# A Trainium2 encoder block: residual seeded into accumulators by ScalarE, and a fourth summed product in two groups of down

## The chip, the cores and the metric

One Trainium2 chip; the kernel uses one of its NeuronCores. Counted is the time of one execution on the device in microseconds. The kernel before took 1141.77 us (median of three runs, 1141.67 to 1141.77).

## What is computed

One layer of an encoder on 256 tokens of width 2048, in fp32:

```python
x = x + jnp.concatenate([out_mla, out_diff], axis=-1) @ w_out[layer]
...
x = x + xo @ w_xo[layer]
hf = rms_norm(x, g_ffn[layer])
x = x + (jax.nn.silu(hf @ w_gate[layer]) * (hf @ w_up[layer])) @ w_down[layer]
return rms_norm(x, g_final)
```

The change touches the two wide products whose result is added onto the residual x: `w_out` (2048 by 2048) and the larger part of `w_down`, called down here (5632 by 2048; the hidden width is taken in one chunk of 512 and five of 1024, numbered 0 to 4 below). x is kept in SBUF as two tiles `x_res` of 128 tokens by 2048.

## The kernel before

**fp32 in three matmuls.** Each operand is split into a rounded high part and a low rest. `mm` (L97 to L101) issues h by h, h by l and l by h, each a matmul with 512 columns, onto one PSUM bank of 128 by 512. Weights come by DMA on SyncE's queue into `wraw` (three buffers). ScalarE casts them to the high part `wh` (L107), VectorE subtracts that from the raw value to give the low part `wl` (L108); `wh` and `wl` have four buffers of 1024 columns each. A buffer is written again only when the last matmul that reads it is done.

**Pairs, P and W.** `wide_project` (L254) multiplies 256 tokens by a block of weights 1024 columns wide; the contracted dimension is taken in pairs of 128 rows. One pair is a 2 by 2 block product. A pair of kind P does it plainly in 8 `mm` (24 matmuls), into four accumulators `accs[tt][oc]`, tt the token tile and oc the block of 512 columns. A pair of kind W uses a scheme with 7 products (21 matmuls): it needs sums of weight blocks (`tsum`, VectorE, L291, L295, L296), split too (the second pair of sums into `wh2` and `wl2`, one buffer each), and sums of activations (`summed_pair`, L237, tiles `forms` and `sums`). Three of its products go straight to accumulators, four into banks Q1, Q5, Q7, Q6, which are summed over all W pairs of a call. The four accumulators and the four Q banks are in two pools of four banks, which swap roles after each call (`banks.reverse()`, L326). The Q pool also serves the transposes `pt` (L504, and L924 in a chunk).

**Leaving and joining.** After the last W of a call, `leave(Q)` (L355) copies Q1 to SBUF on ScalarE (L357) and combines Q1, Q5, Q7, Q6 with the four blocks of x in eight VectorE operations of 128 by 512 (L358 to L365). At the end of the call `join` (L367) adds each accumulator onto x. `wide_add` (L349) is this form, with eight calls: two halves of 1024 columns for w_out; two halves each for three groups of down: chunk 0; chunks 1 and 2; chunks 3 and 4. Gate and up use `wide_result` (L329), which isn't changed.

**Kinds and order.** The two larger groups have eight pairs each: two P and two W from the first chunk (PPWW), and PPPW from the second. They are taken in the order 0, 1, 2, 4, 3, 6, 7, 5, so the W pairs 2, 3 and 7 stand at places 3, 5 and 7. In the second chunk's `wide_chunk` the third pair, being P, is split from the transposes into tiles `hT2`. The very last half-call (`DN_LAST`) takes only five pairs, one of them W; its other weights go through `weights` for a tail of plain products.

**What sets the order.** The program is emitted in the order of a schedule over all engines: each engine gets one static list of instructions and runs it in order, with waits on the other engines. The lists mix casts of weights to come, copies of PSUM and sums of chunks. Line numbers are those of the kernel before, save where the prediction and the order rows below name the changed kernel; there the seeds are L261, the sums of weights L287, L291, L292, the leave L357 to L361, the join L364.

Of the kernel before, what the change touches and what calls it, by code (L numbers as in the profile page):

```python
# [16 lines left out]
ALU = mybir.AluOpType  # L17
# [63 lines left out]
def encoder_block(ctx: ExitStack, tc: tile.TileContext, a, out):  # L81
# [12 lines left out]
    tp = tables.enter_context(tc.tile_pool(name="tp", bufs=1))  # L94


    def mm(o, l, r, start, stop):  # L97

        nc.tensor.matmul(o, l.h, r.h, start=start, stop=False)  # L99
        nc.tensor.matmul(o, l.h, r.l, start=False, stop=False)  # L100
        nc.tensor.matmul(o, l.l, r.h, start=False, stop=stop)  # L101

    last_split, last_cast = [None], [None]

# [146 lines left out]
        split_into(f[:, 4:8, :], s)  # L251
        return Pair(forms=f)

    def wide_project(pairs, src, order, kinds, leave, join, closed=(0, 1), before=None):  # L254

        accs = [[acc_tile() for _ in range(2)] for _ in range(NT)]
        used = [[False] * 2 for _ in range(NT)]
        summed = [i for i in order if kinds[i] == "W"]
        plain = [i for i in order if i not in summed]
        Q = {}
        for n, i in enumerate(order):
            stop = n == len(order) - 1  # L270
            if before is not None:
                before(n)
            raw = pair_raw(src[i])
            if i not in summed:
                w = [split_blocks(raw[:, 2 * k:2 * k + 2, :]) for k in range(2)]
                for tt in range(NT):
                    for oc in range(2):
                        for k in range(2):

                            ends = stop or i == plain[-1] and tt == oc == 1  # L280
                            mm(accs[tt][oc], pairs[i].at(k, tt), w[k][:, oc, :], not used[tt][oc],
                               ends and k == 1 and oc in closed)
                            used[tt][oc] = True
                continue
            if i == summed[0]:
                Q = {q: ps_tile(f"q{q}") for q in (1, 5, 7, 6)}

            b11 = split_blocks(raw[:, 1:3, :])
            if sum_pool:
                t = sum_pool[0].tile([P, 4, 512], F32, name="tsum", tag="tsum", bufs=1)  # L290
                nc.vector.tensor_tensor(out=t[:, 0:2, :], in0=raw[:, 1:3, :],  # L291
                                        in1=raw[:, 0:1, :].to_broadcast([P, 2, 512]), op=ALU.add)  # L292
                t13 = split_blocks(t[:, 0:2, :])
                b21 = split_blocks(raw[:, 3:4, :])
                nc.vector.tensor_tensor(out=t[:, 2, :], in0=t[:, 0, :], in1=raw[:, 2, :], op=ALU.add)  # L295
                nc.vector.tensor_tensor(out=t[:, 3, :], in0=t[:, 2, :], in1=raw[:, 3, :], op=ALU.add)  # L296
# [18 lines left out]
            mm(accs[0][1], S3, b11[:, 1, :], False, stop)  # L315
            mm(Q[5], S5, t1, *own)
            mm(Q[7], S7, t3, *own)
            mm(accs[0][0], A12, b21[:, 0, :], False, stop)
            mm(Q[6], S6, t2, *own)
            mm(accs[1][0], A22, t4, False, stop)  # L320
# [28 lines left out]
    def wide_add(pairs, src, order, kinds, oc0, done=None, closed=(0, 1), before=None):  # L349


        def x(tt, oc):
            return x_res[tt][:, (oc0 + oc) * 512:(oc0 + oc + 1) * 512]

        def leave(Q):  # L355
            v, u = nat("v"), nat("u")
            nc.scalar.copy(out=u, in_=Q[1])  # L357
            nc.vector.tensor_tensor(out=v, in0=Q[6], in1=u, op=ALU.subtract)  # L358
            nc.vector.tensor_tensor(out=x(0, 0), in0=x(0, 0), in1=Q[1], op=ALU.add)
# [12 lines left out]
        return wide_project(pairs, src, order, kinds, leave, join, closed, before)  # L372


    LAT = KVL + DR
# [558 lines left out]
    fss = small.tile([P, NT, 7], F32, name="fss", tag="fss", bufs=1)  # L934
    nc.gpsimd.memset(fss[:, :, 3:4], EPS)

    groups = [([0], (0, 1, 2, 4, 5, 3)), ([1, 2], (0, 1, 2, 4, 3, 6, 7, 5)), ([3, 4], (0, 1, 2, 4, 3, 6, 7, 5))]
    pair0 = 0
    for gi, (chunks, order) in enumerate(groups):
        hp = []  # L940
# [24 lines left out]

        wide_add(hp, src[0], order, kinds, 0, final_square)

        accs = wide_add(hp, src[1], (0, 2, 1, 3, 4), DN_LAST[-8:], 2, closed=(1,))
        summed_up = last_split[0]
        kts = [2 * i + k for i in (5, 6, 7) for k in range(2)]  # L970
        kt = 0
        for p in range(3):
            for w in weights(a["w_down"][0, p]):
                for tt in range(NT):
                    mm(accs[tt][0], xT(kts[kt])[tt], w, False, kt == 5)
# [5 lines left out]
        add_out([accs[tt][0] for tt in range(NT)], 2)  # L981
# [109 lines left out]
```

## Time and profile before

| What | us |
|---|---|
| median of three runs | 1141.77 |
| span of the profiled execution | 1140.2 |
| TensorE busy | 1131.5 |
| VectorE busy | 989.2 |
| ScalarE busy | 651.8 |
| GpSimd busy | 56.2 |

The profile is of one execution. The median is 1.57 us above its span: what lies ahead of the first and behind the last instruction. Times in a timeline are starts, counted from the span's start, followed by the length; a row may stand for several instructions (x2). Successive matmuls overlap, so the cost of one is read from start to start, not from its length.

### The profile page before, as it was taken

Reading aid. Unit: us, or ns where it says so; the run is one execution under the profiler, and the core shown is the slowest. Engines: PE = TensorE matmul, PEld = TensorE weight load, DVE = VectorE, ACT = ScalarE, POOL = GpSimd, SP = SyncE. Lnnn points to the kernel's source line nnn. Section 1 sums busy time; section 2 is a strip of 40 time slices with the busy share of each in tenths; the row PEclk is TensorE's granted clock in tenths of the full one; section 3 lists DMA queues with packets and bytes.
Section 4 is the critical chain, followed back from the end, with each engine's and each line's share of the span. In section 5 each row is a group of like instructions: output and inputs, shape, how many; then the busy total and the mean of one; then the engine's idle time right before and its main releaser. Section 6 shows DMA issues by size and latency. Waiting matters only on the chain.

```text
span 1140.2 us, 14409 instructions
## 1 busy us (share of the span) xinstructions
PE 1131.5 (99%) x5390; PEld 946.1 (83%) x5390; DVE 989.2 (87%) x1354; ACT 651.8 (57%) x933; POOL 56.2 (5%) x75
## 2 busy tenths in 40 slices
PE   9999999999999999999999999999999999999997
PEld 7888888888888888888888888888888888888876
DVE  7788766978997776989899998998999898998996
ACT  6755455556567555665555464564554664664653
POOL 4920000000001000000000000000000000000000
PEclk9999999999999999999999999999999999999999
DMA  9655334546557445455555555555555555565543
GB/s 349 243 196 186 132 118 145 181 142 228 207 209 274 150 156 185 160 210 188 215 191 216 180 198 214 185 195 211 185 202 205 209 197 196 192 243 204 192 170 133
DMA packets 35494, 222.14 MB, mean 195 GB/s; under 512 B 4320, under 2 KB 5600, under 8 KB 11104
## 3 DMA queue, kind: packets, MB, share of 16 engines
q1 hardware_dynamic: 33696, 216.60, 53.5%
q0 software_dynamic: 864, 3.15, 0.8%
q10 hardware_dynamic: 864, 1.47, 0.4%
q8 instruction: 42, 0.69, 0.2%
q14 instruction: 28, 0.23, 0.1%
HBM read 219.11 MB, written 2.10 MB: 194 GB/s over the span
## 4 chain that ended last, share of the span: by engine, by line
PE 98%; issue 0%; ACT 0%; DVE 0%; POOLq 0%; POOL 0%; ACTq 0%
PE acc L99 26%; PE acc L100 26%; PE acc L101 26%; PE q L99 4%; PE q L100 4%; PE q L101 4%; PE pt L504 2%; PE ppt L652 1%; PE psc L100 1%; PE psc L101 1%; PE psc L99 1%; PE acckv L99 0%; PE acckv L101 0%; PE acckv L100 0%; PE pt L924 0%
## 5 line engine op out<-in xcount | busy, mean ns | idle before, releaser
L107 ACT CAST wh<-wraw 128x1024 fp32r<-128x1024 f32 (+2 forms) x401 | 389.3, 989 | 330.4 <-PE acc L101 284.6
L108 DVE TENSOR_TENSOR wl<-wraw,wh 128x1024 fp32r<-128x1024 f32 (+2 forms) x401 | 455.5, 1151 | 82.6 <-ACT wh L107 81.0
L107 ACT CAST wh<-tsum 128x1024 fp32r<-128x1024 f32 (+1 forms) x98 | 98.5, 1007 | 53.4 <-PE acc L101 22.7
L108 DVE TENSOR_TENSOR wl<-tsum,wh 128x1024 fp32r<-128x1024 f32 (+1 forms) x98 | 114.1, 1168 | 13.8 <-ACT wh L107 13.8
L100 PE MATMUL acc<-wl,x2n_h 128*128 128x512 f32 x320 | 124.5, 390 | 0.0
L101 PE MATMUL acc<-wh,x2n_l 128*128 128x512 f32 x320 | 123.9, 389 | 0.0
L99 PE MATMUL acc<-wh,x2n_h 128*128 128x512 f32 x320 | 109.7, 390 | 0.0
L100 PE MATMUL acc<-wl,x0T_h 128*128 128x512 f32 x224 | 88.6, 395 | 0.0
L101 PE MATMUL acc<-wh,x0T_l 128*128 128x512 f32 x224 | 88.2, 394 | 0.0
L99 PE MATMUL acc<-wh,x0T_h 128*128 128x512 f32 x224 | 87.0, 397 | 0.0
L100 PE MATMUL q<-wl,forms_h 128*128 128x512 f32 x191 | 74.4, 390 | 0.0
L101 PE MATMUL q<-wh,forms_l 128*128 128x512 f32 x191 | 74.2, 389 | 0.0
L100 PE MATMUL acc<-wl,hT_h 128*128 128x512 f32 x188 | 73.1, 392 | 0.0
L101 PE MATMUL acc<-wh,hT_l 128*128 128x512 f32 x188 | 72.3, 390 | 0.0
L101 PEld LDWEIGHTS acc<-wh,x2n_l 128*128 128x128 f32 x320 | 60.1, 188 | 12.5
L100 PEld LDWEIGHTS acc<-wl,x2n_h 128*128 128x128 f32 x320 | 60.1, 188 | 12.3
L99 PEld LDWEIGHTS acc<-wh,x2n_h 128*128 128x128 f32 x320 | 59.9, 188 | 12.2
L99 PE MATMUL q<-wh,forms_h 128*128 128x512 f32 x191 | 67.2, 389 | 0.0
L99 PE MATMUL acc<-wh,hT_h 128*128 128x512 f32 x188 | 64.7, 391 | 0.0
L100 PE MATMUL acc<-wl,forms_h 128*128 128x512 f32 x162 | 63.0, 389 | 0.0
L101 PE MATMUL acc<-wh,forms_l 128*128 128x512 f32 x162 | 63.0, 389 | 0.0
L99 PE MATMUL acc<-wh,forms_h 128*128 128x512 f32 x162 | 61.2, 390 | 0.1
(406 smaller groups left out, 2252.6 us busy)
## 6 DMA issues: line engine op xcount, KB each, us to landing
wraw<-in_w_gate SPq DMA_DIRECT2D x44, 1024.0 KB, 4.8
wraw<-in_w_up SPq DMA_DIRECT2D x44, 1024.0 KB, 4.8
wraw<-in_w_dn SPq DMA_DIRECT2D x41, 1024.0 KB, 4.8
wraw<-in_w_in SPq DMA_DIRECT2D x24, 1024.0 KB, 4.8
wraw<-in_w_out SPq DMA_DIRECT2D x16, 1024.0 KB, 4.9
wraw<-in_w_in_lat SPq DMA_DIRECT2D x5, 832.0 KB, 7.1
wraw<-in_w_xk SPq DMA_DIRECT2D x4, 1024.0 KB, 4.9
wraw<-in_w_xq SPq DMA_DIRECT2D x4, 1024.0 KB, 5.0
```

The costliest lines, as they stand in the source:

```text
L99: nc.tensor.matmul(o, l.h, r.h, start=start, stop=False)
L100: nc.tensor.matmul(o, l.h, r.l, start=False, stop=False)
L101: nc.tensor.matmul(o, l.l, r.h, start=False, stop=stop)
L107: last_cast[0] = nc.scalar.copy(out=dst.h, in_=src).ins
L108: last_split[0] = nc.vector.tensor_tensor(out=dst.l, in0=src, in1=dst.h.bitcast(F32), op=ALU.subtract).ins
L504: nc.tensor.transpose(out=pt[:, j * P:(j + 1) * P], in_=src[:, j * P:(j + 1) * P], identity=ident)
L652: nc.tensor.transpose(out=pt[:, kt * S + tt * P:kt * S + (tt + 1) * P], in_=p[:, tt, kt * P:(kt + 1) * P], identity=ident)
```

## The change

`wide_add` hands `wide_project` its four blocks of x as seeds: ahead of a call's first matmul ScalarE copies each into its accumulator, and the matmuls add onto it (no matmul of these calls starts a fresh accumulation on those banks). `leave` then has the copy of Q1 and four VectorE operations, which leave the four combinations in SBUF tiles `left`; `join` adds accumulator and `left` and writes x. The last half-call's plain tail ends in the same `join`.

The kinds of the two larger groups become PPWWPPWW, and their order 0, 2, 1, 3, 4, 6, 7, 5, so the W pairs 2, 3, 6 and 7 stand at places 2, 4, 6 and 7. That makes three more W pairs (both halves of chunks 1 and 2, the first half of chunks 3 and 4), 5381 matmuls for 5390, 32 seed copies, and 32 vector operations fewer in `leave`; `hT2` is gone, and chunks 2 and 4 build the sums of one more pair.

```diff
-DN_KINDS = "PP" + "PPWW" + ("PPWW" + "PPPW") * (NPC // 2)
+DN_KINDS = "PP" + "PPWW" + ("PPWW" + "PPWW") * (NPC // 2)
...
-    def mm(o, l, r, start, stop):
+    def mm(o, l, r, start, stop, seeded=False):
-        nc.tensor.matmul(o, l.h, r.h, start=start, stop=False)
+        nc.tensor.matmul(o, l.h, r.h, start=start, stop=False, skip_group_check=seeded)
...
-    def wide_project(pairs, src, order, kinds, leave, join, closed=(0, 1), before=None):
+    def wide_project(pairs, src, order, kinds, leave, join, closed=(0, 1), before=None, seed=None):
         accs = [[acc_tile() for _ in range(2)] for _ in range(NT)]
-        used = [[False] * 2 for _ in range(NT)]
+        used = [[seed is not None] * 2 for _ in range(NT)]
+        if seed is not None:
+            for tt in range(NT):
+                for oc in range(2):
+                    nc.scalar.copy(out=accs[tt][oc], in_=seed(tt, oc))
...
+        sums = {}
+
         def leave(Q):
-            v, u = nat("v"), nat("u")
-            nc.scalar.copy(out=u, in_=Q[1])
-            nc.vector.tensor_tensor(out=v, in0=Q[6], in1=u, op=ALU.subtract)
-            nc.vector.tensor_tensor(out=x(0, 0), in0=x(0, 0), in1=Q[1], op=ALU.add)
+            for q in ((0, 0), (1, 0), (0, 1), (1, 1)):
+                sums[q] = nat("left")
+            q1, v, u, y = sums.values()
+            nc.scalar.copy(out=q1, in_=Q[1])
+            nc.vector.tensor_tensor(out=v, in0=Q[6], in1=q1, op=ALU.subtract)
             nc.vector.tensor_tensor(out=u, in0=Q[5], in1=v, op=ALU.add)
             nc.vector.tensor_tensor(out=v, in0=v, in1=Q[7], op=ALU.subtract)
-            nc.vector.tensor_tensor(out=x(1, 1), in0=x(1, 1), in1=Q[5], op=ALU.add)
-            nc.vector.tensor_tensor(out=x(0, 1), in0=x(0, 1), in1=u, op=ALU.add)
-            nc.vector.tensor_tensor(out=x(1, 0), in0=x(1, 0), in1=v, op=ALU.subtract)
-            nc.vector.tensor_tensor(out=x(1, 1), in0=x(1, 1), in1=v, op=ALU.add)
+            nc.vector.tensor_tensor(out=y, in0=Q[5], in1=v, op=ALU.add)
 
         def join(tt, oc, acc):
-            nc.vector.tensor_tensor(out=x(tt, oc), in0=x(tt, oc), in1=acc, op=ALU.add)
+            nc.vector.tensor_tensor(out=x(tt, oc), in0=acc, in1=sums[tt, oc],
+                                    op=ALU.subtract if (tt, oc) == (1, 0) else ALU.add)
...
-    groups = [([0], (0, 1, 2, 4, 5, 3)), ([1, 2], (0, 1, 2, 4, 3, 6, 7, 5)), ([3, 4], (0, 1, 2, 4, 3, 6, 7, 5))]
+    groups = [([0], (0, 1, 2, 4, 5, 3)), ([1, 2], (0, 2, 1, 3, 4, 6, 7, 5)), ([3, 4], (0, 2, 1, 3, 4, 6, 7, 5))]
```

In the last three products of a W and in P the new argument is passed to `mm`; the last half-call's `add_out` becomes a loop over `join`.

Three places of the lists are of use below, all in the first half of the group of chunks 1 and 2. In the names the number is that of the tile in its program, so the two programs number alike things differently; q1, q5, q7, q6 are the Q banks, acc the accumulators, and waits names the engines or DMA queues for which a row waits.

ScalarE around the copy of Q1, before:

```order
L107 CAST wh2_7473<-tsum_7461 128x1024 [waits PE_49]
L107 CAST wh_7540<-tsum_7538 128x1024 [waits DVE_49,PE_49,Activation_49]
L357 COPY u_7576<-q1_7376 128x512 [waits PE_49]
L107 CAST wh_7544<-wraw_7532 128x512 [waits PE_49,Activation_49]
L107 CAST wh2_7550<-tsum_7538 128x1024 [waits DVE_49,PE_49,Activation_49]
L107 CAST wh_7588<-wraw_7586 128x1024 [waits DMAHW4_49,PE_49]
L107 CAST wh_7592<-wraw_7586 128x1024 [waits PE_49]
```

and now:

```order
L107 CAST wh2_7537<-tsum_7525 128x1024 [waits DVE_49,Activation_49]
L357 COPY left_7605<-q1_7363 128x512 [waits PE_49]
L261 COPY acc_7652<-xres0_111 128x512 [waits Activation_49]
L107 CAST wh_7570<-tsum_7568 128x1024 [waits DVE_49]
L107 CAST wh_7574<-wraw_7562 128x512
L107 CAST wh_7616<-wraw_7614 128x1024 [waits DMAHW4_49]
L107 CAST wh_7620<-wraw_7614 128x1024 [waits PE_49]
L107 CAST wh2_7580<-tsum_7568 128x1024 [waits DVE_49,PE_49]
```

The seed of the first accumulator of the next half (acc_7652, first block of x) now stands directly behind the copy, and behind it the casts of the last W's sums and of the P that follows; the cast for wh2 has moved from behind the copy to ahead of it for one W, and far behind it for the next.

TensorE from the last matmul onto Q1, before:

```order
L101 MATMUL q1_7376<-wh_7534,forms_l_7288 128x512
L100 MATMUL acc_7303<-wl_7535,forms_h_7287 128x512
L101 MATMUL acc_7303<-wh_7534,forms_l_7288 128x512
L100 MATMUL q6_7379<-wl2_7474,forms_h_6596 128x512 [waits DVE_49]
L101 MATMUL q6_7379<-wh2_7473,forms_l_6597 128x512
L100 MATMUL acc_7304<-wl2_7474,forms_h_6596 128x512
L101 MATMUL acc_7304<-wh2_7473,forms_l_6597 128x512
L99 MATMUL acc_7304<-wh_7500,hT2h_7253 128x512
L100 MATMUL acc_7304<-wl_7501,hT2h_7253 128x512
L101 MATMUL acc_7304<-wh_7500,hT2l_7254 128x512
L99 MATMUL acc_7304<-wh_7504,hT2h_7253 128x512
L100 MATMUL acc_7304<-wl_7505,hT2h_7253 128x512
```

and now:

```order
L101 MATMUL q1_7363<-wh_7564,forms_l_7305 128x512
L100 MATMUL acc_7320<-wl_7565,forms_h_7304 128x512
L101 MATMUL acc_7320<-wh_7564,forms_l_7305 128x512
L100 MATMUL q6_7366<-wl2_7538,forms_h_7289 128x512 [waits DVE_49]
L101 MATMUL q6_7366<-wh2_7537,forms_l_7290 128x512
L100 MATMUL acc_7321<-wl2_7538,forms_h_7289 128x512
L101 MATMUL acc_7321<-wh2_7537,forms_l_7290 128x512
L99 MATMUL q5_7364<-wh_7570,forms_h_7304 128x512 [waits Activation_49]
L99 MATMUL q7_7365<-wh_7570,forms_h_7304 128x512
L99 MATMUL acc_7319<-wh_7574,forms_h_7304 128x512 [waits Activation_49]
L99 MATMUL acc_7320<-wh_7616,hT_h_7259 128x512 [waits Activation_49]
L99 MATMUL acc_7322<-wh_7616,hT_h_7259 128x512
```

Two W pairs now run interleaved here. Between the last matmul onto Q1 and the first use of the casts behind the copy (wh_7570, wh_7574, wh_7616; before wh_7544, still after these rows) there are six, eight and nine matmuls.

TensorE between two uses of the single wh2 buffer, before, where the next wh2 tile (wh2_7473) comes 24 matmuls after the last reader of wh2_7396:

```order
L99 MATMUL q6_7379<-wh2_7396,forms_h_6581 128x512 [waits DVE_49]
L100 MATMUL q6_7379<-wl2_7397,forms_h_6581 128x512
L101 MATMUL q6_7379<-wh2_7396,forms_l_6582 128x512
L99 MATMUL acc_7302<-wh_7467,forms_h_6596 128x512 [waits Activation_49]
L100 MATMUL acc_7302<-wl_7468,forms_h_6596 128x512 [waits DVE_49]
```

and now, with wh2_7383 and wh2_7460:

```order
L99 MATMUL q7_7365<-wh_7450,forms_h_6604 128x512
L100 MATMUL q7_7365<-wl_7451,forms_h_6604 128x512
L101 MATMUL q7_7365<-wh_7450,forms_l_6605 128x512
L99 MATMUL q6_7366<-wh2_7383,forms_h_6589 128x512 [waits DVE_49]
L100 MATMUL q6_7366<-wl2_7384,forms_h_6589 128x512
L101 MATMUL q6_7366<-wh2_7383,forms_l_6590 128x512
L99 MATMUL q1_7363<-wh_7521,forms_h_7289 128x512 [waits Activation_49]
L99 MATMUL acc_7320<-wh_7521,forms_h_7289 128x512
L99 MATMUL q6_7366<-wh2_7460,forms_h_6604 128x512 [waits Activation_49]
```

The products of pair 2 onto q7 and q6 have moved to directly ahead of those of pair 3 and of the next W.

More of the change, by code (lines that the diff above doesn't have):

```diff
@@ L94, in encoder_block @@
     tp = tables.enter_context(tc.tile_pool(name="tp", bufs=1))
-    def mm(o, l, r, start, stop):
-        nc.tensor.matmul(o, l.h, r.h, start=start, stop=False)
-        nc.tensor.matmul(o, l.h, r.l, start=False, stop=False)
-        nc.tensor.matmul(o, l.l, r.h, start=False, stop=stop)
+    def mm(o, l, r, start, stop, seeded=False):
+        nc.tensor.matmul(o, l.h, r.h, start=start, stop=False, skip_group_check=seeded)
+        nc.tensor.matmul(o, l.h, r.l, start=False, stop=False, skip_group_check=seeded)
+        nc.tensor.matmul(o, l.l, r.h, start=False, stop=stop, skip_group_check=seeded)
     last_split, last_cast = [None], [None]
@@ L281, in wide_project @@
                             mm(accs[tt][oc], pairs[i].at(k, tt), w[k][:, oc, :], not used[tt][oc],
-                               ends and k == 1 and oc in closed)
+                               ends and k == 1 and oc in closed, seed is not None)
                             used[tt][oc] = True
@@ L314, in wide_project @@
             mm(Q[1], A11, b11[:, 0, :], *own)
-            mm(accs[0][1], S3, b11[:, 1, :], False, stop)
+            mm(accs[0][1], S3, b11[:, 1, :], False, stop, seed is not None)
             mm(Q[5], S5, t1, *own)
             mm(Q[7], S7, t3, *own)
-            mm(accs[0][0], A12, b21[:, 0, :], False, stop)
+            mm(accs[0][0], A12, b21[:, 0, :], False, stop, seed is not None)
             mm(Q[6], S6, t2, *own)
-            mm(accs[1][0], A22, t4, False, stop)
+            mm(accs[1][0], A22, t4, False, stop, seed is not None)
             if i == summed[-1]:
@@ L353, in x @@
             return x_res[tt][:, (oc0 + oc) * 512:(oc0 + oc + 1) * 512]
+        sums = {}
         def leave(Q):
-            v, u = nat("v"), nat("u")
-            nc.scalar.copy(out=u, in_=Q[1])
-            nc.vector.tensor_tensor(out=v, in0=Q[6], in1=u, op=ALU.subtract)
-            nc.vector.tensor_tensor(out=x(0, 0), in0=x(0, 0), in1=Q[1], op=ALU.add)
+            for q in ((0, 0), (1, 0), (0, 1), (1, 1)):
[3 more added lines that the diff above has]
+            nc.vector.tensor_tensor(out=v, in0=Q[6], in1=q1, op=ALU.subtract)
             nc.vector.tensor_tensor(out=u, in0=Q[5], in1=v, op=ALU.add)
             nc.vector.tensor_tensor(out=v, in0=v, in1=Q[7], op=ALU.subtract)
-            nc.vector.tensor_tensor(out=x(1, 1), in0=x(1, 1), in1=Q[5], op=ALU.add)
-            nc.vector.tensor_tensor(out=x(0, 1), in0=x(0, 1), in1=u, op=ALU.add)
-            nc.vector.tensor_tensor(out=x(1, 0), in0=x(1, 0), in1=v, op=ALU.subtract)
-            nc.vector.tensor_tensor(out=x(1, 1), in0=x(1, 1), in1=v, op=ALU.add)
+            nc.vector.tensor_tensor(out=y, in0=Q[5], in1=v, op=ALU.add)
         def join(tt, oc, acc):
-            nc.vector.tensor_tensor(out=x(tt, oc), in0=x(tt, oc), in1=acc, op=ALU.add)
+            nc.vector.tensor_tensor(out=x(tt, oc), in0=acc, in1=sums[tt, oc],
+                                    op=ALU.subtract if (tt, oc) == (1, 0) else ALU.add)
             if done is not None:
                 done(tt, oc0 + oc)
-        return wide_project(pairs, src, order, kinds, leave, join, closed, before)
+        accs = wide_project(pairs, src, order, kinds, leave, join, closed, before, x)
+        return accs, join
     LAT = KVL + DR
@@ L966, in encoder_block @@
         wide_add(hp, src[0], order, kinds, 0, final_square)
-        accs = wide_add(hp, src[1], (0, 2, 1, 3, 4), DN_LAST[-8:], 2, closed=(1,))
+        accs, join = wide_add(hp, src[1], (0, 2, 1, 3, 4), DN_LAST[-8:], 2, closed=(1,))
         summed_up = last_split[0]
@@ L974, in encoder_block @@
                 for tt in range(NT):
-                    mm(accs[tt][0], xT(kts[kt])[tt], w, False, kt == 5)
+                    mm(accs[tt][0], xT(kts[kt])[tt], w, False, kt == 5, True)
                 kt += 1
@@ L980, in encoder_block @@
                     final_gain(tt, oc)
-        add_out([accs[tt][0] for tt in range(NT)], 2)
+        for tt in range(NT):
+            join(tt, 0, accs[tt][0])
         for tt in range(NT):
```

## Prediction

> **What bounds the kernel now.** First the page: its span, the engines' shares, the granted clock in 40 slices and the chain that ended last.
>
> ```profile
> span 1140.2 us, 14409 instructions
> PE 1131.5 (99%) x5390; PEld 946.1 (83%) x5390; DVE 989.2 (87%) x1354; ACT 651.8 (57%) x933; POOL 56.2 (5%) x75
> PEclk9999999999999999999999999999999999999999
> PE 98%; issue 0%; ACT 0%; DVE 0%; POOLq 0%; POOL 0%; ACTq 0%
> ```
>
> TensorE works without pause at full clock, so a matmul taken out pays in full, and a wait put in costs in full. Nothing else is late by more than fractions of a microsecond. The profiled span is 1140.2 us; the median of the three runs is 1141.77 us, so 1.57 us lie outside the span, and I add all changes to 1141.77.
>
> Next the busy time by stage, for the stages that gain summed products: 793 to 838 us holds most of down's first half in the group of chunks 1 and 2, 838 to 882 what follows it, 1046 to 1097 the same place in the last group.
>
> ```profile
> core 0: us, PE busy (x) PEld busy (x) DVE busy (x) ACT busy (x) POOL busy (x), PEclk, DMA share, GB/s
> 793.00:838.00 45.00, 45.00 (x208) 37.35 (x207) 42.37 (x55) 26.35 (x33) 0.00 (x0) 1.00 0.56 198
> 838.00:882.00 44.00, 44.00 (x196) 36.44 (x195) 40.42 (x48) 21.40 (x23) 0.00 (x0) 1.00 0.53 193
> 1046.00:1097.00 51.00, 50.89 (x233) 41.95 (x232) 48.38 (x63) 29.31 (x39) 0.00 (x0) 1.00 0.48 173
> ```
>
> VectorE is busy for 42.37 of 45 and 48.38 of 51 us: 2.6 us of room in each. ScalarE has room on average, but its queue is in order: what stands behind a waiting copy waits too.
>
> The prices come from the timeline around the copy of Q1 in the first of these stages: TensorE, then ScalarE, then VectorE.
>
> ```profile
> 824.48 0.39 PE L100 MATMUL q<-wl,forms_h 128*128 128x512 f32 x1
> 824.71 0.39 PE L101 MATMUL q<-wh,forms_l 128*128 128x512 f32 x1
> 824.93 0.39 PE L100 MATMUL acc<-wl,forms_h 128*128 128x512 f32 x1
> 825.16 0.39 PE L101 MATMUL acc<-wh,forms_l 128*128 128x512 f32 x1
> ```
>
> ```profile
> 825.13 0.59 ACT L357 COPY u<-q 128x512 f32<-128x512 f32 x1 [0.65 <-PE q L101]
> 825.64 0.62 ACT L107 CAST wh<-wraw 128x512 fp32r<-128x512 f32 x1
> 826.54 1.05 ACT L107 CAST wh<-tsum 128x1024 fp32r<-128x1024 f32 x1 [0.27 <-DVE xres L359]
> 827.50 3.95 ACT L107 CAST wh<-wraw 128x1024 fp32r<-128x1024 f32 x4
> ```
>
> ```profile
> 819.70 1.22 DVE L108 TENSOR_TENSOR wl<-wraw,wh 128x1024 fp32r<-128x1024 f32 x1
> 820.84 1.22 DVE L108 TENSOR_TENSOR wl<-tsum,wh 128x1024 fp32r<-128x1024 f32 x1
> 824.07 0.69 DVE L296 TENSOR_TENSOR tsum<-tsum,wraw 128x512 f32<-128x512 f32 x1
> 824.68 1.22 DVE L108 TENSOR_TENSOR wl<-tsum,wh 128x1024 fp32r<-128x1024 f32 x1
> 825.82 0.68 DVE L359 TENSOR_TENSOR xres<-xres,q 128x512 f32<-128x512 f32 x1
> 826.42 0.68 DVE L108 TENSOR_TENSOR wl<-wraw,wh 128x512 fp32r<-128x512 f32 x1
> 827.62 1.23 DVE L108 TENSOR_TENSOR wl<-tsum,wh 128x1024 fp32r<-128x1024 f32 x1 [0.52 <-ACT wh L107]
> ```
>
> Read from start to start: a matmul 0.227; on ScalarE 0.51 for 512 columns (825.13 to 825.64) and 0.96 for 1024 (826.54 to 827.50, 1.05 to its end); on VectorE 0.60 for 512 (825.82 to 826.42) and 1.14 for 1024 (819.70 to 820.84, 1.22 to its end). From the last matmul onto Q1 (824.71) to ScalarE's copy (825.13) pass 0.42, and from a cast's start (826.54) to VectorE's low part (827.62) 1.08. So a buffer of 1024 columns that TensorE lets go is used again at the earliest 0.42 + 1.05 + about 0.05 = 1.53 us after the start of its last reader.
>
> **The change, part by part.**
>
> *Nine matmuls fewer.* Three pairs go from 24 to 21 matmuls each: 9 x 0.227 = **-2.04 us**, if nothing is late.
>
> *Four vector adds fewer in each of eight calls.* Each call sheds 4 x 0.60 = 2.4 us of VectorE. In most stages TensorE doesn't wait for it, and this is worth nothing. In w_out's second half it does wait:
>
> ```profile
> 327.65 0.39 PE L101 MATMUL q<-wh,forms_l 128*128 128x512 f32 x1
> 327.88 0.61 PE L99 MATMUL acc<-wh,mT_h 128*128 128x512 f32 x2
> 328.68 0.50 PE L100 MATMUL acc<-wl,mT_h 128*128 128x512 f32 x1 [0.19 <-DVE wl L108]
> 329.01 0.39 PE L101 MATMUL acc<-wh,mT_l 128*128 128x512 f32 x1
> ```
>
> ```profile
> 326.81 0.68 DVE L359 TENSOR_TENSOR xres<-xres,q 128x512 f32<-128x512 f32 x1
> 327.40 1.22 DVE L108 TENSOR_TENSOR wl<-wraw,wh 128x1024 fp32r<-128x1024 f32 x1
> ```
>
> Four matmuls take 1.36 us instead of 0.91, because the low part of 327.40 stands behind L359. That add goes, the low part comes 0.60 earlier: **-0.45 us**. Next late there would be the cast of the same weight, but the two matmuls from 327.88 on already run from it.
>
> *The copy of Q1 ahead of a cast, in the last half.* There the trace already shows what a ScalarE queue behind the Q1 copy can do:
>
> ```profile
> 1093.78 0.39 PE L101 MATMUL q<-wh,forms_l 128*128 128x512 f32 x1
> 1095.59 0.39 PE L101 MATMUL acc<-wh,hT_l 128*128 128x512 f32 x1
> 1095.82 0.99 PE L99 MATMUL acc<-wh,forms_h 128*128 128x512 f32 x2
> 1096.65 0.40 PE L99 MATMUL q<-wh,forms_h 128*128 128x512 f32 x1
> ```
>
> ```profile
> 1094.20 0.59 ACT L357 COPY u<-q 128x512 f32<-128x512 f32 x1 [3.04 <-PE q L101]
> 1094.68 0.62 ACT L107 CAST wh<-wraw 128x512 fp32r<-128x512 f32 x1
> 1095.20 1.05 ACT L107 CAST wh<-tsum 128x1024 fp32r<-128x1024 f32 x1
> ```
>
> Copy, cast and cast end at 1096.25, and the matmul pair at 1095.82 takes 0.83 instead of 0.45. In the changed order this second cast (wh2_9794) stands ahead of the copy, so it isn't held: **-0.38 us**. So far -2.87 us.
>
> *32 seed copies on ScalarE.* No copy from SBUF to PSUM by ScalarE is in the trace. The nearest row is the opposite direction, in the view of that line:
>
> ```profile
> L357 ACT COPY u<-q x8: 574/587/589, 277.4 to 1094.2; 128x512 f32<-128x512 f32 x8
> ```
>
> I take 0.51 in a queue, as from 825.13 to 825.64; the bounds are 0.3 (half) and 0.7. The Trainium skill's "ScalarE: Activation LUTs" (What ACT_TABLE_LOAD costs) gives an instruction with immediates 186 ns + 0.833 ns a column, less about 93 ns back to back: by that page an estimated 613 and 520 ns at 512 columns, against the 587 and 0.51 us here. Its tip that ScalarE reaches PSUM faster than SBUF speaks for the lower bound; no run here shows it yet, and by it the sum would be at most some 0.4 us lower.
>
> A seed costs where TensorE waits for what is queued behind it. Most of the 32 stand behind the join that frees their value and 1 to 2 us or more ahead of their first matmul: nothing. One in each of the two large groups does not: acc_7652 and acc_9730, the seed of the first accumulator of the next half, directly behind the Q1 copy.
>
> *That place, counted from the start of the last matmul onto Q1 (time 0).* Before, behind the copy stood a 512-column cast used only 15 matmuls (3.4 us) on. Now: copy from 0.42 to 0.93, seed to 1.44, then wh_7570 (ends 2.49), wh_7574 (starts 2.40, with 512 columns ends 3.0), wh_7616 (starts 2.91, ends 3.96). TensorE reaches their first matmuls at 7, 9 and 10 x 0.227 = 1.59, 2.04 and 2.27. So it waits 0.9, then hardly, then 0.75: **+1.7 us**, of which 0.5 is the seed. The same rows stand in the last group (wh_9640, wh_9644, wh_9686): **+1.7 us** again.
>
> *The first W, now second in the order, is held.* Its products Q7 and Q6 wait for chunk 2's sums, since their PSUM pool holds the transposes until these are read, and so come just ahead of those of the second W. That pair's wh2_7460 needs the single wh2 buffer, whose last reader is the last matmul of q6 from wh2_7383; TensorE asks for wh2_7460 three matmuls later, 0.68 us, where 1.53 are needed: **+0.85 us** a group, so +1.7. Before, 24 matmuls (5.4 us) lay between, and it was free. A low part on VectorE at the same place (wl_7488) may add up to 0.5 us a group; I leave it to the range.
>
> *VectorE's queue in the group of chunks 1 and 2.* A W instead of a P adds 1.14 + 2 x 0.60 for the sums of weights and 1.14 + 0.60 for low parts: 4.08 us. The extra form costs an estimated 1.4 (from 0.60 and 1.14 by width: 0.2 for 128 and 0.33 for 256 columns; four sums and 1024 columns of low parts against 512). Less the 2.4 of the adds this is +3.1 us in each first half, while TensorE's work shrinks by 0.68: 42.37 + 3.1 = 45.5 against 44.3 us. Row by row: wl_7571 starts at 1.44 + 1.08 = 2.52; with it to wl_7701 stand seven of 1024 columns (7 x 1.14), six of 512 (6 x 0.60) and the last (1.22): ready at 15.3. TensorE asks for it after 53 matmuls, 12.0. So 3.3 late in all, 1.7 of which it has waited already: **+1.6 us**. The last group's counterpart comes to 14.7 against 60 matmuls, 13.6: covered by the wait of 1.7. In the second halves the addition is 4.08 - 2.4 = 1.7 against 3.6 us of room: nothing.
>
> *Joins, DMAs, outputs.* Four joins a call stay; they now read seed-fed accumulators and a left tile, same width. Weights are the same transfers, and the queues' order around them the same: nothing. The tail behind the last matmul is unchanged.
>
> **Sum:** -2.87 + 2 x 1.7 + 2 x 0.85 + 1.6 = +3.8 us: 1141.77 + 3.8 = **1145.5 us**.
>
> **The rivals.** A difference below 0.2% (2.28 us) can't be told from none here.
>
> *No new wait decides (faster).* If these casts are ready in time, only the savings remain: 1141.77 - 2.87 = 1138.9 us. For it: TensorE was never held in these stages before, and ScalarE is half idle (26.35 of 45). Against it: the waits come from the order of an in-order queue, and the rows at 1095.82 show one. It decides if the three casts behind the copy wait for nothing TensorE needs within 2.3 us, or TensorE is already later than VectorE there for another reason. Chance 0.12.
>
> *Only the waits on ScalarE, not VectorE's queue (no change).* VectorE could reach wl_7701 in time if it enters the stage with more room, shed in earlier calls: -2.87 + 5.1 = 1144.0 us, and with seeds at 0.3 us 1143.5. Chance 0.20.
>
> *VectorE bounds both groups (slower still).* The 2.6 us of idling in each window are waits for casts; if they stay, the windows need 42.37 + 2.6 + 3.1 = 48.1 against 44.3 and 54.1 against 50.3 us: +3.8 in each, 1141.77 - 2.87 + 7.6 = 1146.5, and with 0.5 us a group for wl_7488 and the late casts of the next half up to 1149. Chance 0.14.
>
> *The clock falls in the pauses.* If a pause lets the granted clock drop to a half for as long again as it lasted, the pauses of 1.7, 1.6, 1.7 and twice 0.85 us cost half their 6.7 us more: 1148.9 us. For it, nothing: the clock stands at 1.00 in every window. The Trainium skill's "TensorE: Matmul & The Clock Gate" (What's actually happening) drops the clock after an idle window of about 3.4 us; none of these pauses is that long, so by it this doesn't happen. Chance 0.04.
>
> **How the numbers follow.** The forecast itself has 0.50, from 1144.1 to 1147.5 us: seeds of 0.3 take 0.4 off, wl_7488 adds up to 1.0, VectorE's term may be 0.5 to 2.2. The range leaves out the faster case and the ends of the two slowest: 1142.0 to 1148.5 us. Faster 0.12; the second rival is "same", 0.20; the rest, 0.68, is slower.
>
> **What would show it.** Right: TensorE pauses of some 0.9 and 0.75 us right behind the last matmul onto Q1 in both large groups, released by ScalarE's casts; 0.85 at the second W's first matmul from wh2; a pause for a low part at the start of the second half in the first group only; none at 328 and 1095.8 us any more; seeds of about 0.59 us. Wrong: no pauses there, or pauses in places that I held free (w_out, chunk 0's group, the second halves), or a clock under 1.00.

## The result and the profile after

The changed kernel takes **1153.29 us** (median of four runs, 1152.99 to 1153.82), against 1141.77 us: a ratio of 1.0101, 95% interval 1.0088 to 1.0113. It was forecast slower at 1145.5 us with a range up to 1148.5: the way was right, but the change is about three times as large as forecast and lies beyond the range. The span of the profiled execution grew from 1140.2 to 1151.4 us.

The page of the changed kernel, the same lines as before:

```profile
span 1151.4 us, 14427 instructions
PE 1133.1 (98%) x5381; PEld 942.8 (82%) x5381; DVE 989.0 (86%) x1347; ACT 673.7 (59%) x975; POOL 57.9 (5%) x75
PEclk9999999999999999999999999999999999999999
PE 92%; DVE 4%; ACT 2%; issue 1%; DMA 1%; POOLq 0%; POOL 0%; DVEq 0%; ACTq 0%
```

Nine matmuls fewer, and VectorE's busy time over the whole is the same (989.2 before, 989.0 now): what the shorter leave saved, the fourth W took. The chain that ended last is no longer TensorE's alone; VectorE has 4% and ScalarE 2% of it. What TensorE waited for, by the view of its waits:

```profile
PE q L99 <- ACT wh L107: 3.9, 6, 0.9
PE q L100 <- DVE wl L108: 2.0, 1, 2.0
PE acc L99 <- ACT acc L261: 1.9, 2, 1.1
...
PE acc L100 <- DVE wl L108: 0.9, 2, 0.6
PE acc L99 <- ACT wh L107: 0.9, 2, 0.5
```

The columns are the total, the times and the longest. This view counts idle time between matmuls whose ends are modelled; what a wait costs is read from start to start, less 0.227 us for each matmul. The timeline of TensorE shows where, in the first half of the group of chunks 1 and 2:

```profile
813.78 0.51 PE L100 MATMUL acc<-wl,hT_h 128*128 128x512 f32 x1 [0.30 <-DVE wl L108]
...
819.65 0.40 PE L99 MATMUL acc<-wh,forms_h 128*128 128x512 f32 x1
820.66 0.50 PE L99 MATMUL q<-wh,forms_h 128*128 128x512 f32 x1 [0.62 <-ACT wh L107]
...
824.89 0.40 PE L99 MATMUL acc<-wh,forms_h 128*128 128x512 f32 x1
825.73 0.50 PE L99 MATMUL q<-wh,forms_h 128*128 128x512 f32 x1 [0.44 <-ACT wh L107]
...
829.72 0.39 PE L101 MATMUL acc<-wh,forms_l 128*128 128x512 f32 x1
831.02 0.73 PE L99 MATMUL q<-wh,forms_h 128*128 128x512 f32 x2 [0.92 <-ACT wh L107]
831.60 0.45 PE L99 MATMUL acc<-wh,forms_h 128*128 128x512 f32 x1
832.50 0.73 PE L99 MATMUL acc<-wh,hT_h 128*128 128x512 f32 x2 [0.45 <-ACT wh L107]
...
842.15 0.39 PE L99 MATMUL q<-wh,forms_h 128*128 128x512 f32 x1
844.58 0.50 PE L100 MATMUL q<-wl,forms_h 128*128 128x512 f32 x1 [2.05 <-DVE wl L108]
844.92 0.39 PE L101 MATMUL q<-wh,forms_l 128*128 128x512 f32 x1
```

From 844.58 to 844.92 are 0.34 us: the matmul behind a wait takes 0.11 more than its 0.227, at every wait of this list. With that, the waits here cost 0.91 (for low parts, around 813), 0.78 + 0.11, 0.61 + 0.11, 1.07 + 0.11, 0.67 + 0.11 and 2.20 + 0.11: 6.8 us. The last group has the first five too, from 1070 to 1092 us (4.9 us, with 1.28 for the low parts), and another at its second half. That one and one in w_out wait for seeds:

```profile
287.44 0.39 PE L99 MATMUL acc<-wh,mixT_h 128*128 128x512 f32 x1
288.58 0.50 PE L99 MATMUL acc<-wh,mixT_h 128*128 128x512 f32 x1 [0.74 <-ACT acc L261]
...
1100.78 0.39 PE L99 MATMUL q<-wh,forms_h 128*128 128x512 f32 x1
1102.32 0.50 PE L99 MATMUL acc<-wh,hT_h 128*128 128x512 f32 x1 [1.15 <-ACT acc L261]
```

They cost 0.91 + 0.11 and 1.31 + 0.11 us. ScalarE's timeline shows what stood ahead of the first of the two: two casts, then a mean square (L206) that needs the join of the half before, then the seed.

```profile
285.42 2.00 ACT L107 CAST wh<-wraw 128x1024 fp32r<-128x1024 f32 x2 [1.21 <-issue]
287.33 0.62 ACT L206 ACTIVATE junk<-xres 128x512 bf16<-128x512 f32 x1
287.86 0.18 ACT L206 ACTIVATION_READ_ACCUMULATOR junk<-xres 128x1 f32 x1
287.95 0.57 ACT L261 COPY acc<-xres 128x512 f32<-128x512 f32 x1
```

All together: 6.8 + 6.3 for the groups, 1.0 + 0.3 in w_out (0.27 ahead of the seed's wait, at 280 us), less 2.0 for the matmuls and 0.5 + 0.4 for the old waits at 328 and 1095.8 us, which are gone: +11.5, against 11.2 us of span. The waits are where the extra time is; the experiments ask why they are there.

### The profile page after: what moved, and what is told of

The parts are those of the page before. It is cut to its first block, busy times and chain, and to the rows that moved or that the text cites. A ratio compares the mean times of both kernels' runs of the same rounds, so it can differ in the third digit from the quotient of the medians.

```text
span 1151.4 us, 14427 instructions
## 1 busy us (share of the span) xinstructions
PE 1133.1 (98%) x5381; PEld 942.8 (82%) x5381; DVE 989.0 (86%) x1347; ACT 673.7 (59%) x975; POOL 57.9 (5%) x75
## 4 chain that ended last, share of the span: by engine, by line
PE 92%; DVE 4%; ACT 2%; issue 1%; DMA 1%; POOLq 0%; POOL 0%; DVEq 0%; ACTq 0%
PE acc L99 24%; PE acc L100 24%; PE acc L101 24%; PE q L100 4%; PE q L101 4%; PE q L99 4%; DVE wl L108 2%; PE pt L502 2%; ACT wh L107 1%; DMA wraw<-in_w_dn 1%; DVE tsum L287 1%; PE ppt L650 1%; PE psc L100 1%; PE psc L101 1%; PE psc L99 1%
## 5 line engine op out<-in xcount | busy, mean ns | idle before, releaser
L107 ACT CAST wh<-tsum 128x1024 fp32r<-128x1024 f32 (+1 forms) x104 | 104.2, 1009 | 61.7 <-PE acc L101 24.3
L108 DVE TENSOR_TENSOR wl<-tsum,wh 128x1024 fp32r<-128x1024 f32 (+1 forms) x104 | 120.8, 1168 | 14.1 <-ACT wh L107 13.7
L100 PE MATMUL q<-wl,forms_h 128*128 128x512 f32 x203 | 79.0, 390 | 2.0 <-DVE wl L108 2.0
L101 PE MATMUL q<-wh,forms_l 128*128 128x512 f32 x203 | 78.8, 389 | 0.0
L99 PE MATMUL q<-wh,forms_h 128*128 128x512 f32 x203 | 72.3, 393 | 3.9 <-ACT wh L107 3.9
L100 PE MATMUL acc<-wl,forms_h 128*128 128x512 f32 x175 | 68.1, 391 | 0.1
L101 PE MATMUL acc<-wh,forms_l 128*128 128x512 f32 x175 | 67.6, 389 | 0.0
L99 PE MATMUL acc<-wh,forms_h 128*128 128x512 f32 x175 | 66.9, 392 | 0.0
```

The costliest lines, as they stand in the source:

```text
L99: nc.tensor.matmul(o, l.h, r.h, start=start, stop=False, skip_group_check=seeded)
L100: nc.tensor.matmul(o, l.h, r.l, start=False, stop=False, skip_group_check=seeded)
L101: nc.tensor.matmul(o, l.l, r.h, start=False, stop=stop, skip_group_check=seeded)
L107: last_cast[0] = nc.scalar.copy(out=dst.h, in_=src).ins
L108: last_split[0] = nc.vector.tensor_tensor(out=dst.l, in0=src, in1=dst.h.bitcast(F32), op=ALU.subtract).ins
```

## The experiments

**First theory**, that of the prediction: the new order and kinds put waits into the in-order queues at particular places (behind the copy of Q1, at the one wh2 buffer). **Second**: VectorE's work bounds the groups. **Third**: the seeds themselves hold ScalarE and TensorE.

The lists of every run are emitted anew from its own schedule. An edit therefore also moves rows that it doesn't name, and no run has exactly the order of the change.

**Seeds alone.** The old kinds and order, the rest of the change kept:

```diff
-DN_KINDS = "PP" + "PPWW" + ("PPWW" + "PPWW") * (NPC // 2)
+DN_KINDS = "PP" + "PPWW" + ("PPWW" + "PPPW") * (NPC // 2)
-    groups = [... ([1, 2], (0, 2, 1, 3, 4, 6, 7, 5)), ([3, 4], (0, 2, 1, 3, 4, 6, 7, 5))]
+    groups = [... ([1, 2], (0, 1, 2, 4, 3, 6, 7, 5)), ([3, 4], (0, 1, 2, 4, 3, 6, 7, 5))]
```

> The seeds, the shorter leave and the new join, with the old kinds (three W pairs of eight) and the old order. First theory (the time is lost in waits that the new kinds and order put into the in-order queues of ScalarE and VectorE; seeds cost only where one stands late): the seed wait at w_out's second half (1.0 us) stays, the two old pauses at 328 and 1095.8 us go, so 1141.0 to 1143.5 us. Second theory (VectorE's total work bounds the groups): less work than before, so at most 1141.5 us. Third theory (the seed copies themselves hold ScalarE and TensorE): most of the 11.5 us stays, 1148 us or more.

Measured 1141.86 us, ratio 1.0001 (0.9992 to 1.0011): no change. The third theory falls, and the second's "at most 1141.5" is missed by 0.4 us. 32 seeds and 32 vector operations fewer, VectorE's busy time down from 989.2 to 973.5 us, and nothing gained: TensorE wasn't waiting for it. The late seed in w_out is there (1.0 us, at 289) and eats what the old two waits give back.

**Fourth W and order alone.** The kernel before with only these two lines changed, without seeds:

> The fourth W and the new order, with the old leave, join and no seeds. First theory: the waits at the early W, at the wh2 buffer, at the sums and behind the copy of Q1 stay, each without the 0.5 us of the seed, and the late seeds (1.0 and 1.4 us) go: 1148 to 1151 us. Second theory: VectorE has 2.4 us more to do in each call than in the changed kernel, so slower than 1153 us, up to 1158. Third theory: without seeds only the saved matmuls count, 1139 to 1142 us.

Measured 1151.31 us, ratio 1.0084 (1.0069 to 1.0099): just above the first theory's 1151. So most of the loss is with the fourth W or its order. The second theory, as stated, expected slower than 1153. It misses: VectorE does 15.6 us more here than in the change (1004.6 for 989.0) and the kernel is 2.0 us faster. The adds that the leave sheds are worth little; in the half shown above, seven of the eight operations of the long leave come behind the W pairs, from 840 us on.

**The old order with four W:**

```diff
-    groups = [... ([1, 2], (0, 2, 1, 3, 4, 6, 7, 5)), ([3, 4], (0, 2, 1, 3, 4, 6, 7, 5))]
+    groups = [... ([1, 2], (0, 1, 2, 4, 3, 6, 7, 5)), ([3, 4], (0, 1, 2, 4, 3, 6, 7, 5))]
```

> The changed kernel with the groups' old order 0, 1, 2, 4, 3, 6, 7, 5; seeds and the fourth W stay, so the matmuls and VectorE's work are those of the changed kernel. First theory: the pauses that come from the W at place 2 (some 0.9 to 1.3 for low parts, 0.9 for wh2, 0.7 for the sums, in each group) go, one or two waits behind the copy of Q1 stay: 1146 to 1149 us. Second and third theory: the same work and the same seeds, so still 1152 to 1154 us.

Measured 1153.44 us, ratio 1.0103 (1.0088 to 1.0118): the first theory misses, by 4 us and more; the second and third expected 1152 to 1154. TensorE's waits by this view:

```profile
PE q L99 <- ACT wh L107: 5.3, 7, 1.2
PE acc L99 <- ACT acc L261: 1.9, 2, 1.1
PE acc L99 <- ACT wh L107: 1.3, 3, 0.5
...
PE q L100 <- DVE wl L108: 1.1, 2, 0.5
```

The waits of the early W are gone, and others, of the same sum, are in places that were free.

**Two buffers for wh2:**

```diff
-        pool, tags, bufs = (wp, ("wh", "wl"), 4) if pool is None else (pool, ("wh2", "wl2"), 1)
+        pool, tags, bufs = (wp, ("wh", "wl"), (4, 4)) if pool is None else (pool, ("wh2", "wl2"), (2, 1))
```

> The changed kernel with two buffers for the tile wh2 (wl2 still one). First theory: the pause of 0.90 us a group at the first use of wh2 goes, everything else stays: 1151.0 to 1152.0 us, unless the wait for the sums behind it grows by the same amount. Second and third theory: no change, 1153 us.

Measured 1152.07 us, ratio 1.009 (1.0073 to 1.0107): about 1.2 us less than the change, just short of the 1.3 to 2.3 that the first theory expected. The wait of 0.90 for wh2 went, but just behind its place TensorE now waits 0.68 us for a low part, so only 0.2 us a group is gained there; the rest comes from other places of the new lists.

**Alternating pairs.** The first theory in a mended form, that W pairs side by side are the trouble, and a **new theory** against it:

```diff
-    groups = [... ([1, 2], (0, 2, 1, 3, 4, 6, 7, 5)), ([3, 4], (0, 2, 1, 3, 4, 6, 7, 5))]
+    groups = [... ([1, 2], (0, 2, 1, 3, 4, 6, 5, 7)), ([3, 4], (0, 2, 1, 3, 4, 6, 5, 7))]
```

> The changed kernel with the groups' order 0, 2, 1, 3, 4, 6, 5, 7, so that P and W alternate throughout; work and seeds as in the changed kernel. First theory in its mended form (W pairs that stand next to each other, 6 and 7 here, 4, 3, 6, 7 in the run with the old order, ask for too much at once; spread out, they fit): the waits behind the copy of Q1 go, 1147 to 1149.5 us. New theory (a fourth W doesn't fit in any order: for each W, VectorE has to add the sums of weights in its queue, between low parts whose casts wait for TensorE to let a buffer go, and ScalarE's casts wait for the sums; the round trips add up to more than TensorE's time for the pairs): 1152.5 to 1154 us.

Measured 1154.15 us, ratio 1.0106 (1.0091 to 1.0121): just above the new theory's 1152.5 to 1154, and far from the first's. The two waits behind the copy of Q1 went; those at 814, 821 and 826 us stayed, and four new ones stand in the second half's first pairs, two of them for seeds.

**Without the sums of weights:**

```diff
-            if sum_pool:
+            if sum_pool and len(order) == 8 and seed is not None:
+                t13 = split_blocks(raw[:, 0:2, :])
+                b21 = split_blocks(raw[:, 3:4, :])
+                t24 = split_blocks(raw[:, 2:4, :], sum_pool[0])
+            elif sum_pool:
```

> The changed kernel, which leaves out the sums of weight blocks in the W pairs of the two large groups and casts the raw blocks in their place (so another product is computed); matmuls, casts, low parts, seeds, order of the pairs stay. New theory: the waits in these groups go with the sums, only the seed's wait in w_out stays: 1139 to 1141 us. First theory (order and copies): at least the waits behind the copy of Q1 and at wh2 stay, 1144 to 1148 us. Third theory (seeds): 1151 us or more.

Measured 1140.3 us, ratio 0.9986 (0.9977 to 0.9996): all of the loss is gone, though copies of Q1, seeds, casts and low parts are as many as in the change. Of TensorE's waits only one seed's is left beside two that were there before:

```profile
PE wps L388 <- DVE warm L382: 1.2, 1, 1.2
PE acc L99 <- ACT acc L261: 0.7, 1, 0.7
PE po L99 <- ACT val_h L113: 0.2, 1, 0.2
```

**The sums added, but not used**, to part the time of the sums from the wait for them:

```diff
-                t13 = split_blocks(t[:, 0:2, :])
+                t13 = split_blocks(raw[:, 0:2, :] if len(order) == 8 and seed is not None else t[:, 0:2, :])
...
-                t24 = split_blocks(t[:, 2:4, :], sum_pool[0])
+                t24 = split_blocks(raw[:, 2:4, :] if len(order) == 8 and seed is not None else t[:, 2:4, :], sum_pool[0])
```

> The changed kernel, in which VectorE still adds the sums of weight blocks in the two large groups, but the casts take the raw blocks instead (so another product is computed). If it is the wait of ScalarE's casts for the sums that costs (a chain through both engines), the time comes down nearly as far as without the sums, 1140.5 to 1143 us. If it is VectorE's time for them (2.3 us for each W, in a queue that is full while the W pairs run), most of the loss stays: 1149 to 1152.5 us.

Measured 1153.6 us, ratio 1.0105 (1.0091 to 1.0119): no part of the loss goes; it is above even the 1149 to 1152.5 that was expected if VectorE's time costs. So it is VectorE's time for the sums, not ScalarE's wait for their results; that part of the new theory's round trips is not the cause. What is left is the second theory: VectorE's work bounds the stretch in which the W pairs run. As each run has lists of its own, their order is a rival, but an unlikely one: all seven kernels that have the fourth W in both groups and spend the time for all its sums lie between 1150.7 and 1154.2 us, in whatever order.

The windows from 793 to 845 us hold the first half's pairs. They give the busy time of TensorE, its weight loads, VectorE and ScalarE; first the kernel before:

```profile
793.00:845.00 52.00, 52.00 (x239) 43.14 (x238) 49.37 (x64) 28.35 (x35) 0.00 (x0) 1.00 0.51 182
```

the change, and the change with the sums unused:

```profile
793.00:845.00 52.00, 47.18 (x208) 36.71 (x207) 48.74 (x65) 30.68 (x40) 0.00 (x0) 1.00 0.49 180
793.00:845.00 52.00, 48.84 (x215) 37.83 (x213) 48.72 (x66) 29.95 (x39) 0.00 (x0) 1.00 0.51 182
```

and the change without the sums:

```profile
793.00:845.00 52.00, 52.00 (x239) 43.18 (x238) 43.14 (x58) 32.51 (x44) 0.00 (x0) 1.00 0.51 181
```

VectorE gives no more busy time in the change than before, 48.7 for 49.4 us, and TensorE does 208 instead of 239 matmuls meanwhile. Without the sums VectorE needs 43.1 us and TensorE is full. But VectorE isn't busy throughout either: 3.3 us of the 52 are idle in the change, 2.0 of them in one piece. VectorE's row there, and the cast on ScalarE for which it waits:

```profile
819.29 1.23 DVE L108 TENSOR_TENSOR wl<-wraw,wh 128x1024 fp32r<-128x1024 f32 x1 [1.99 <-ACT wh L107]
818.20 1.05 ACT L107 CAST wh<-wraw 128x1024 fp32r<-128x1024 f32 x1 [1.62 <-PE q L101]
```

The cast waits for TensorE to let go of a buffer. So VectorE loses time there for want of buffers, and TensorE waits for its results afterwards.

**Without the sums of one W of four:**

```diff
+            if sum_pool and len(order) == 8 and i == 6 and seed is not None:
...
```

> The changed kernel without the sums for one of the four W pairs of each large group (pair 6, whose casts take raw blocks, so another product is computed): VectorE has then 2.3 us less to do in each of the three first and second halves that have four W. If VectorE's time in these stretches decides, part of the 11.5 us goes, two to three microseconds a group and not all: 1146 to 1149 us. If only the full number of sums matters as a chain, or the seeds do, 1151 us or more.

Measured 1147.3 us, ratio 1.005 (1.0036 to 1.0064): 6.0 us less than the change, for sums taken out of three half-calls. More work of VectorE, more loss, in steps.

**Forms only.** Seeds, three W and the old order, but the forms for pair 6 are built and then used plainly (its weights lie packed for a W, so other blocks are multiplied):

```diff
-                wide_add(hp, src[h], order, kinds, 2 * h)
+                wide_add(hp, src[h], order, kinds if not gi else "PPWWPPPW", 2 * h)
-        wide_add(hp, src[0], order, kinds, 0, final_square)
+        wide_add(hp, src[0], order, "PPWWPPPW", 0, final_square)
```

> Seeds, three W pairs and the old order, but chunks 2 and 4 build the forms of one more pair, which is then taken plainly. If the additional sums of activations and their low parts on VectorE (some 1.4 us in each first half) are what doesn't fit: 1144 us or more. New theory: they fit into VectorE's room, as it has room before the W pairs come: 1141.5 to 1142.8 us.

Measured 1142.17 us, ratio 1.0003 (0.9994 to 1.0013). The 1.4 us of sums of activations fit, beside three W. In the last group's stretch VectorE is busy for 51.1 of 52 us here, and TensorE full:

```profile
1046.00:1098.00 52.00, 52.00 (x238) 42.94 (x238) 51.13 (x70) 34.09 (x49) 0.00 (x0) 1.00 0.50 177
```

So a high share of VectorE by itself doesn't hold TensorE; what matters is presumably whether the work that TensorE asks for next is among what is left in VectorE's list.

**Seeds in down only**, with the old leave in w_out's two calls (`seeded=False` there):

> The changed kernel, with the calls of w_out as before (no seeds there, the long leave). New and first theory: the wait for a late seed in w_out's second half (0.9 + 0.1 us) and the 0.27 us before it go, the old one at 328 us (0.46 us) comes back: 0.8 us less, 1152.5 us, and less by 1 to 2 us more if the order that follows moves work away from the start of the second half (wait of 2.3 us). Third theory (every seed costs some of ScalarE's time): eight of 32 seeds fewer, a quarter of 11.5 us less, 1150.5 us, with waits shorter in all places.

Measured 1150.69 us, ratio 1.0075 (1.0058 to 1.0092): 2.6 us less than the change, which doesn't part first and third theory by itself. The waits in the trace do. The waits at 280 and 288 us are gone and the old one at 328 is back; the five waits in each group are there at the same lengths, while in place of the one of 2.3 us at the second half's start there are pauses of at most 0.3: TensorE's list there has seven other matmuls ahead of the one that waited. The late seed of the last group is still there (1.15 by the view). So a seed costs where it is late, and through the list that is emitted with it; the second was not tested by itself.

**One group:**

```diff
-DN_KINDS = "PP" + "PPWW" + ("PPWW" + "PPWW") * (NPC // 2)
+DN_KINDS = "PP" + "PPWW" + ("PPWW" + "PPWW" + "PPWW" + "PPPW")
-    groups = [... ([3, 4], (0, 2, 1, 3, 4, 6, 7, 5))]
+    groups = [... ([3, 4], (0, 1, 2, 4, 3, 6, 7, 5))]
```

> The changed kernel with the fourth W and the new order only in the group of chunks 1 and 2; chunks 3 and 4 keep three W and the old order. New theory: each group pays for itself, and the last group's waits (6.3 us) go against three matmuls more (0.7 us): 1147 to 1148.5 us. If the delay were handed on from one group to the next, or came from the seeds: 1150 us or more.

Measured 1149.58 us, ratio 1.0064 (1.0049 to 1.008), its runs at 1147.70, 1149.53, 1149.63 and 1150.01. Above the new theory's 1148.5, but the last group has no wait left, so each group does pay for itself. The trace has a reason for the rest, in TensorE's timeline:

```profile
842.66 0.39 PE L99 MATMUL q<-wh,forms_h 128*128 128x512 f32 x1
845.03 0.50 PE L100 MATMUL q<-wl,forms_h 128*128 128x512 f32 x1 [1.99 <-DVE wl L108]
...
846.38 0.63 PE L99 MATMUL acc<-wh,hT_h 128*128 128x512 f32 x1
846.81 0.63 PE L100 MATMUL acc<-wl,hT_h 128*128 128x512 f32 x1
```

and in the windows of 1 us there, the granted clock third from the end:

```profile
846.00:847.00 1.00, 1.00 (x5) 0.74 (x4) 1.00 (x2) 0.20 (x1) 0.00 (x0) 0.61 0.00 0
847.00:848.00 1.00, 1.00 (x4) 0.80 (x3) 1.00 (x3) 0.00 (x0) 0.00 (x0) 0.50 0.00 0
848.00:849.00 1.00, 1.00 (x4) 0.71 (x3) 1.00 (x2) 0.00 (x0) 0.00 (x0) 0.50 0.00 0
849.00:850.00 1.00, 1.00 (x5) 0.82 (x4) 1.00 (x2) 0.77 (x2) 0.00 (x0) 0.68 0.00 0
```

Matmuls stand 0.43 apart instead of 0.227: the clock was at a half for 3.4 us after the wait, which cost 1.7 us. The run at 1147.70 seems to be one without it: its mean granted clock is on record as 0.998, that of the other three as 0.997, 0.996 and 0.997, and 3.4 us at a half lower the mean by 0.0015.

**A W where VectorE has room.** Seeds, the old kinds and order in down, and a third W in w_out's first half:

```diff
-OUT_KINDS, OUT_ORDERS = ("PPPPWWPP", "PPPPWWWP"), ((0, 1, 2, 3, 4, 6, 5, 7), (0, 1, 2, 4, 3, 5, 7, 6))
+OUT_KINDS, OUT_ORDERS = ("PPPPWWWP", "PPPPWWWP"), ((0, 1, 4, 2, 5, 3, 6, 7), (0, 1, 2, 4, 3, 5, 7, 6))
```

> Seeds, the old kinds and order in down, but a third W pair in the first half of w_out, in alternation with P (order 0, 1, 4, 2, 5, 3, 6, 7). VectorE has room there, 35.4 of 42 us busy in the profile before, so a W should pay its 0.68 us where the forms exist already; the alternation may take the wait for a seed away too: 1140.5 to 1141.5 us, faster than both kernels by a little. If a W never pays on this kernel: 1142 us or more.

Measured 1141.96 us, ratio 1.0002 (0.9994 to 1.0011): no gain, against an expected 1140.5 to 1141.5. Its profiled span is 1139.4 against 1140.2 us, but it is that of the fastest of eleven runs. The wait for the seed is gone; transposes of the attention's output wait 0.86 us for VectorE instead, at 257 us. No version that computes the layer was found to beat the kernel before by more than runs can tell.

## Why the prediction was right in direction and wrong in size

- **Nine matmuls, 2.04 us; the waits at 328 and 1095.8 us.** As forecast: 5381 matmuls, both waits gone, the first back where w_out's old leave is back.
- **The seed's price.** 584 ns, taken as 587; in a queue 0.52 (829.41 to 829.93 us), taken as 0.51. The view of the seeds' line:

```profile
L261 ACT COPY acc<-xres x32: 573/584/597, 214.4 to 1105.8; 128x512 f32<-128x512 f32 x32
```

The copies of Q1, from PSUM to SBUF, have a median of 584 ns as well, so the faster way to PSUM that the Trainium skill's "ScalarE: Activation LUTs" (its tip on destinations) promises doesn't show at this width. The two copies differ in their source too, so this is no clean test of the destination.
- **"Nothing" for all other seeds** failed twice: 1.0 us in w_out, 1.4 us in the last group (and 0.3 just ahead of the first). I had counted their distance to the first matmul, and not the mean square or the casts ahead of them in ScalarE's queue.
- **Behind the copy of Q1, 1.7 us a group.** 1.18 + 0.78 measured, each with 0.11 behind the wait. **At wh2, 0.85.** 0.90 measured. **VectorE's list at the second half, 1.6.** 2.3 measured, there in the first group alone, as forecast; with the lists of the run with seeds in down only it was gone, so its place is one of the list.
- **Missed:** 0.72 us a group for casts behind late sums (825.73), and 0.9 and 1.3 for low parts, left to the range at 0.5 a group. By terms, 7.7 us are missing between the forecast and the measurement: 2.7 for late seeds and the 0.3, 2.2 for low parts, 1.4 for casts behind late sums, 0.7 at the second half, 0.6 behind the copy of Q1 and at wh2.
- **The step that failed** is VectorE's term. I set its additional 3.1 us a first half against 2.6 us of room, charged the excess at the one place that I could count (1.6 us, first group) and let waits on ScalarE "cover" it in the last. The 2.6 us weren't room. In the kernel before, VectorE's idle time from 793 to 838 us is four waits for casts (0.40, 0.97, 0.63 and 0.52 us); in the change it still idles for 3.3 us in 52 and gives no more busy time than before. So the added work was late in more places than one, and TensorE lost 6.8 and 6.3 us in the two groups instead of 4.2 and 2.6. Of the waits that I priced, those at wh2 and behind the copy of Q1 were real, but when one was taken away (order, buffer) waits came back elsewhere; with the sums they went together. The rival "VectorE bounds both groups" had the mechanism, and had named these waits for casts; I gave it a chance of 0.14 and 1146.5 to 1149 us, too little as well.
- **The clock rival** didn't happen in the change: its profile has the clock at 1.00 through the waits, also behind the one of 2.2 us at 842 to 844. In the run with one group the clock fell after a wait of 2.1 us. The Trainium skill's "TensorE: Matmul & The Clock Gate" (What's actually happening) speaks of an idle window of about 3.4 us; here a shorter pause was enough, and the slow stretch lasted 3.4 us.

What stays open is the size. The rival's sum, with VectorE's idle time staying as it is, gives 3.8 us a group; if the leave's 2.4 us count for nothing, as the run without seeds suggests, 6.2 us. Both are estimates from the prediction's prices. Measured are 6.8 us in the first group and, beside the late seed, 4.9 in the last. No window of busy time in the record turns VectorE's added work into these numbers.

## What to carry to other kernels

An engine's idle time isn't room while it is a wait for another engine: ask of each gap what ended it before counting it. Here 2.6 us of gaps were waits for casts, and they were still there when more work came. Price a trade per unit of work on every engine: here a W takes 4.1 us more of VectorE than a P for 0.7 us less of TensorE, which pays only where VectorE can take that much on the spot. And when a wait that is removed comes back elsewhere with the same sum, stop mending places and look for the engine that all of them wait for, directly or through another.

## What the runs showed of the hardware

- The matmul behind a wait starts its successor 0.34 us later instead of 0.227 (820.66 to 821.00, 844.58 to 844.92 us): each wait of TensorE in these rows costs 0.11 us over its length.
- TensorE's clock fell to a half for 3.4 us after a wait of 2.1 us in the run with one group; in the change it stayed at 1.00 after one of 2.2 us.
- Matmuls add onto values that ScalarE has put into PSUM, and show no cost of their own for it: behind the seed's wait in the last group they start 0.23 us apart (1102.65 to 1102.88), as elsewhere.
